# Weight buffers that start 96 bytes apart, and every second weight tile taken in pieces of 256 columns

## The chip, the core and the metric

The kernel runs on one core of a Trainium2 chip. The metric is the device time of one launch in microseconds (us), the median of three runs. A profile of one further execution is read beside it: it records every instruction on TensorE (PE, and PEld for its weight loads), VectorE (DVE), ScalarE (ACT), GpSimd (POOL) and the DMAs that SyncE (SP) issues.

## What is computed

Two layers over 512 tokens of width 1024. Each layer projects the normed tokens into three branches (a latent attention, a state-space scan and an attention over the keys that a top-256 of index scores picks), gates and merges them, and adds a per-layer embedding:

```python
for i in range(DEPTH):                                   # DEPTH = 2
    h = rms_norm(x, norm_g[i])
    (c_q, c_kv, ..., merge_logits) = jnp.split(h @ w_in[i], split_at, axis=-1)
    o_a = mla_branch(...) * jax.nn.silu(gate_a)
    o_b = ssd_branch(...)
    o_c = dsa_branch(...) * jax.nn.silu(gate_c)          # lax.top_k(index_score, 256) inside
    g_a, g_b, g_c = jnp.split(jax.nn.sigmoid(merge_logits), 3, axis=-1)
    merged = g_a * (o_a @ w_br_a[i]) + g_b * (o_b @ w_br_b[i]) + g_c * (o_c @ w_br_c[i])
    x = x + merged @ w_out[i]
    x = x + jax.nn.sigmoid(x @ w_ple_gate[i]) * (p[i] @ w_ple[i])
return rms_norm(x, final_norm)
```

## The kernel before

**The products with weights.** Features lie on partitions, the 512 tokens along the free axis. A unit of weights (128 x 1024 numbers, 512 KB) is fetched by `wload` (L214 to L228) into a buffer `raw`; ACT rounds it to `hi` (L226) and DVE takes the rest, `lo` = raw - hi (L227). Activations are split into `hi` and `lo` the same way. `mm` (L230) makes one tile of results: for each of its k blocks of 128 rows it multiplies hi by hi (L237) and lo by hi (L238), and then hi by lo (L245), all into one PSUM tile. A tile with eight blocks is 24 matmuls, each a 128 x 128 block of weights that stays in the array and 512 token columns that stream past it. Each matmul brings a weight load of its own. In rows, `p<-s,wh` means: into PSUM tile p, streaming s, with wh in the array.

**How much of it there is.** `mm` makes 250 tiles, 244 of 512 columns and six of 256 (the last three `pgate` tiles of layer 1, in two halves each). They are 4,932 of the 7,004 matmuls of the program; `three` (L675) makes another 144 of the same kind without `mm`. The others are the attentions' logits (L779 to L781, L883, L884), their transposes (L563) and products with values (L602), the index scores (L840, L841), the scan (L1009, L1047, L1071, L1076) and small ones.

**The order.** PE's order is the order in which the code is written. `weave` (L487) runs an attention or the scan step by step, and after each step takes some of the tiles' matmuls, four at a time (`CHUNK`), so that PE has work while DVE and ACT do a softmax. The first part of a layer, up to the end of the scan, is such a mixture. After the scan come the last gates, 8 tiles of `br_b`, 8 of `w_out` and 8 of `pgate`, and there tile follows tile with hardly anything between (in the profile from 587 to 740 us and from 1285 to 1432 us). The order on DVE, ACT, POOL and SP is made by a scheduler that puts each instruction where, by its own estimate of times, it could start; `wload`'s three instructions are given priority (`AHEAD`). The buffers are handed out in turn: three `hi`, three `lo`, two `raw` (`WB`).

**The top-256.** `topk` (L854) takes 16 rounds of MAX (L861) and MATCH_REPLACE (L864) on DVE for three blocks of queries, then makes masks (L868). The sparse attention `dsa` needs these masks from its second block on; meanwhile PE runs tiles.

**Places in memory.** All activation tiles are 2,048 bytes a partition and all weight buffers 4,096, and all of them begin at a multiple of 512 bytes. `vc`, the values of the sparse attention (stationary in L602, `p<-s,vc`), begins 160 bytes past one; the other attention's values are ordinary activation tiles (L602, `p<-s,s`).

Of the kernel before, what the change touches and what calls it, by code (L numbers as in the profile page):

```python
# [26 lines left out]
F32R = mybir.dt.float32r  # L27
# [5 lines left out]
L, D, T = 2, 1024, 512  # L33
# [125 lines left out]
class Build:  # L159
    def __init__(self, tc, I, out, ctx, dbg=None):  # L160
        self.tc, self.nc, self.I, self.out, self.dbg = tc, tc.nc, I, out, dbg or {}
        pool = lambda name, **k: ctx.enter_context(tc.tile_pool(name=name, **k))

        self.front = pool("front", bufs=1)
        self.slots = pool("slots", bufs=1)
        self.wp = pool("wp", bufs=2)
        self.const = pool("const", bufs=1)
        self.small = pool("small", bufs=6)
        PS = bass.MemoryType.PSUM
        self.psum = pool("psum", bufs=2, space=PS)  # L170
        self.dram = pool("dram", bufs=1, space=bass.MemoryType.DRAM)
        self.free_slots = deque(range(NSLOT))
        self.todo = deque()
        self.of = {}
        self.n = 0
        self.ahead = 0
        self.fetched = {}
        self.chunk = CHUNK
        self.peak = 0


    def slot(self, dt=F32, shape=(128, 512)):
        i = self.free_slots.popleft()
        self.peak = max(self.peak, NSLOT - len(self.free_slots))
        self.n += 1
# [28 lines left out]
    def wload(self, l, name):  # L214
        if (l, name) in self.fetched:
            return self.fetched.pop((l, name))
        nc = self.nc
        kind, (cols,) = UNITS[UIDX[name]]
        n = 640 if kind == "uq" else _KT[kind] * len(cols)
        hi = self.wp.tile([128, 1024], F32R, name=f"wh{self.n}", tag="whi", bufs=WB[0])  # L220
        lo = self.wp.tile([128, 1024], F32R, name=f"wl{self.n}", tag="wlo", bufs=WB[1])
        raw = self.wp.tile([128, 1024], F32, name=f"wr{self.n}", tag="raw", bufs=WB[2])
        self.n += 1
        with self.tc.high_priority(offset=self.ahead):
            nc.sync.dma_start(raw[:, :n], self.I["w"][l, UIDX[name], :, :n])
            nc.scalar.activation(hi[:, :n], raw[:, :n], AF.Copy)  # L226
            nc.vector.tensor_sub(lo[:, :n], raw[:, :n], hi[:, :n].bitcast(F32))  # L227
        return hi, lo  # L228

    def mm(self, ps, w, off, acts, t=slice(0, T)):  # L230

        nc = self.nc
        hi, lo = w
        n, cost = len(acts), 0
        for k, (ah, al) in enumerate(acts):
            c = slice(off + 128 * k, off + 128 * k + 128)
            nc.tensor.matmul(ps[:, t], hi[:, c], ah[:, t], start=k == 0, stop=False)  # L237
            nc.tensor.matmul(ps[:, t], lo[:, c], ah[:, t], start=False, stop=False)  # L238
            cost += 2
            if cost >= self.chunk:  # L240
                yield cost
                cost = 0
        for k, (ah, al) in enumerate(acts):
            c = slice(off + 128 * k, off + 128 * k + 128)
            nc.tensor.matmul(ps[:, t], hi[:, c], al[:, t], start=False, stop=k == n - 1)  # L245
            cost += 1
            if cost >= self.chunk or k == n - 1:
                yield cost
                cost = 0
# [885 lines left out]
    def layer(self, l, xs, s):  # L1135
# [117 lines left out]

        for m in range(8 - LAST):
            self.pgate(l, m, x1, x1p)
            self.stat_add(s, x1[m], m == 0)
        ws = [self.wload(l, ("pgate", m)) for m in range(8 - LAST, 8)]
        rest = deque()

        def tail(half):  # L1260
# [3 lines left out]
            with self.tc.high_priority(offset=URGENT):  # L1264
                self.pgate(l, 7, x1, x1p, ws[LAST - 1], t)
                nc.scalar.activation(q[:, t], x1[7][:, t], AF.Square)
# [5 lines left out]
        for half in range(2):  # L1272
            t = slice(256 * half, 256 * half + 256)
            for m in range(8 - LAST, 7):
                self.pgate(l, m, x1, x1p, ws[m - 8 + LAST], t)
                self.stat_add(s, x1[m], False, t)
                if half and m == 8 - LAST:
                    R = self.stat_rows(y, range(2))
# [57 lines left out]
REL = (1, 3, 4, 4)  # L1336
WB = (3, 3, 2)
NSLOT = 80
LAST = 3
CHUNK = 4  # L1340
FIRST = (("c_kv", 0), ("c_kv", 1), "C")
# [36 lines left out]
```

## Time and profile before

| | |
|---|---|
| median of three runs (lowest to highest) | 1455.37 us (1454.93 to 1456.69) |
| the profiled execution, its own time | 1455.85 us |
| its span, first to last instruction | 1454.0 us |
| PE, PEld busy | 1410.4 us (97%), 1153.9 us (79%) |
| DVE, ACT, POOL busy | 1092.3 us (75%), 718.8 us (49%), 150.2 us (10%) |
| mean granted TensorE clock | 0.994 of 2.4 GHz |

Busy times of PE are to be read with care: matmuls overlap in the pipeline and their ends are modelled, so that a busy PE need not be at its best. What one matmul costs is the distance between the starts of two that follow each other. A number in square brackets in a row is the idle time of that engine before the instruction, with what ended it.

### The profile page before, as it was taken

To read this page: it belongs to the slowest core of one execution; us is meant where nothing else is said; L and a number is where in the kernel's file an instruction comes from. 1 tells how busy PE (TensorE), PEld (TensorE's weight loads), DVE (VectorE), ACT (ScalarE), POOL (GpSimd) and SP (SyncE) were. 2 spreads that over 40 slices of the span, in tenths; PEclk is the share of its full clock that TensorE was granted. 3 is DMA by queue.
4 is the path that set the end of the run, shared out by engine and by line. 5 is a ranking of instruction groups with operands and counts; after the bars stand their busy time and mean duration, and the time that the engine had idled before them with its cause. 6 is when DMAs were issued, how large, how long until landed. Compare 5 with 4: busy or idle time off the path is not lost.

```text
span 1454.0 us, 20141 instructions
## 1 busy us (share of the span) xinstructions
PE 1410.4 (97%) x7252; PEld 1153.9 (79%) x7252; DVE 1092.3 (75%) x2234; ACT 718.8 (49%) x1367; POOL 150.2 (10%) x140
## 2 busy tenths in 40 slices
PE   6999999998999999999999999999999999999997
PEld 4878877787878778888888888888788777788886
DVE  7668786996888997664565697889888798765545
ACT  7557678525656442432345576632466544342332
POOL 1000000031120221000001000000322122110000
PEclk9999999999999999999999999999999999999998
DMA  7442332433333322543444322323333333244331
GB/s 258 145 130 72 92 97 78 133 103 99 112 113 115 118 80 77 160 153 104 130 160 129 94 75 76 95 91 101 109 105 116 105 115 100 73 132 152 108 101 59
DMA packets 67609, 162.39 MB, mean 112 GB/s; under 512 B 9237, under 2 KB 21653, under 8 KB 67509
## 3 DMA queue, kind: packets, MB, share of 16 engines
q1 hardware_dynamic: 67509, 161.11, 35.5%
q8 instruction: 57, 0.93, 0.3%
q14 instruction: 43, 0.35, 0.1%
HBM read 142.27 MB, written 13.83 MB: 107 GB/s over the span
## 4 chain that ended last, share of the span: by engine, by line
PE 73%; DVE 18%; ACT 3%; issue 3%; DMA 1%; POOL 1%; SPq 0%; POOLq 0%; DVEq 0%; ACTq 0%
PE p L245 20%; PE p L237 19%; PE p L238 19%; DVE wl L227 3%; PE p L602 3%; PE p L563 2%; DVE s L864 2%; DVE s L1034 2%; DVE m L861 2%; ACT wh L226 1%; DVE s L966 1%; DMA s<-cum_d 1%; DVE s L1037 1%; PE p L683 1%; PE p L687 1%
## 5 line engine op out<-in xcount | busy, mean ns | idle before, releaser
L237 PE MATMUL p<-s,wh 128*128 128x512 f32 (+1 forms) x1644 | 650.5, 397 | 9.0 <-ACT wh L226 7.9
L238 PE MATMUL p<-s,wl 128*128 128x512 f32 (+1 forms) x1644 | 637.9, 389 | 1.2 <-DVE wl L227 1.2
L245 PE MATMUL p<-s,wh 128*128 128x512 f32 (+1 forms) x1644 | 425.5, 391 | 0.0
L226 ACT ACTIVATE wh<-wr 128x1024 fp32r<-128x1024 f32 (+2 forms) x214 | 223.6, 1045 | 330.7 <-PE p L245 214.0
L237 PEld LDWEIGHTS p<-s,wh 128*128 128x128 f32 x1644 | 311.3, 189 | 69.6 <-ACT wh L226 7.9
L238 PEld LDWEIGHTS p<-s,wl 128*128 128x128 f32 x1644 | 311.1, 189 | 61.1 <-DVE wl L227 2.6
L245 PEld LDWEIGHTS p<-s,wh 128*128 128x128 f32 x1644 | 300.6, 189 | 59.9 <-issue 2.8
L227 DVE TENSOR_TENSOR wl<-wr,wh 128x1024 fp32r<-128x1024 f32 (+2 forms) x214 | 263.4, 1231 | 108.8 <-ACT wh L226 107.8
L553 ACT ACTIVATE s<-s,m 128x128 f32<-128x128 f32 (+3 forms) x128 | 71.5, 559 | 68.9 <-DVE m L552 68.5
L572 ACT ACTIVATE s<-p 128x256 fp32r<-128x256 f32 (+1 forms) x192 | 65.8, 343 | 56.1 <-PE p L563 27.7
L573 DVE TENSOR_TENSOR s<-p,s 128x256 fp32r<-128x256 f32 (+1 forms) x192 | 71.6, 374 | 14.1 <-ACT s L572 12.7
L881 POOL TENSOR_TENSOR s<-s,s 128x256 f32<-128x256 f32 (+2 forms) x48 | 57.7, 1216 | 134.0 <-DMA s<-bias_d 84.7
L563 PE MATMUL p<-c,s 128*128 128x128 f32 x320 | 56.6, 274 | 7.9 <-DVE s L555 7.9
L563 PEld LDWEIGHTS p<-c,s 128*128 128x128 f32 x320 | 40.4, 140 | 25.4 <-issue 12.8
L1130 DVE SCALAR_TENSOR_TENSOR s<-s,p 128x512 f32<-128x512 f32 x48 | 32.4, 676 | 32.6 <-PE p L245 32.6
L410 ACT ACTIVATE s<-s 128x512 f32<-128x512 f32 (+1 forms) x42 | 25.3, 610 | 63.7 <-DVE s L1097 39.8
L555 DVE TENSOR_SCALAR s<-s,m 128x128 f32<-128x128 f32 (+3 forms) x128 | 52.3, 409 | 2.6
L966 DVE SCALAR_TENSOR_TENSOR s<-p,v,s 128x511 f32<-128x511 f32 (+2 forms) x72 | 53.2, 739 | 0.0
L864 DVE MATCH_REPLACE8 s<-m,s 128x256 f32<-128x256 f32 (+2 forms) x96 | 51.3, 538 | 0.0
L431 POOL TENSOR_TENSOR m<-m,v 128x4 f32<-128x4 f32 (+1 forms) x10 | 12.5, 1247 | 368.4 <-DVE m L430 368.3
L881 POOL TENSOR_TENSOR s<-s,c 128x128 f32<-128x128 f32 x16 | 11.0, 693 | 374.6 <-DMA s<-bias_d 204.4
L861 DVE MAX8 m<-s 128x8 f32<-128x256 f32 (+2 forms) x96 | 49.0, 543 | 0.0
(188 smaller groups left out, 1688.3 us busy)
## 6 DMA issues: line engine op xcount, KB each, us to landing
wr<-in_w_dram SPq DMA_DIRECT2D x204, 512.0 KB, 3.5
s<-cum_d SPq DMA_DIRECT2D x32, 256.0 KB, 3.7
s<-in_x_dram SPq DMA_DIRECT2D x16, 256.0 KB, 4.7
ple_d<-s SPq DMA_DIRECT2D x16, 256.0 KB, 4.0
s<-bias_d SPq DMA_DIRECT2D x16, 256.0 KB, 3.3
s<-ple_d SPq DMA_DIRECT2D x13, 256.0 KB, 2.7
s<-bias_d SPq DMA_DIRECT2D x16, 192.0 KB, 2.7
s<-s SPq DMA_DIRECT2D x44, 64.0 KB, 2.0
```

Source lines behind the costliest of these rows:

```text
L226: nc.scalar.activation(hi[:, :n], raw[:, :n], AF.Copy)
L227: nc.vector.tensor_sub(lo[:, :n], raw[:, :n], hi[:, :n].bitcast(F32))
L237: nc.tensor.matmul(ps[:, t], hi[:, c], ah[:, t], start=k == 0, stop=False)
L238: nc.tensor.matmul(ps[:, t], lo[:, c], ah[:, t], start=False, stop=False)
L245: nc.tensor.matmul(ps[:, t], hi[:, c], al[:, t], start=False, stop=k == n - 1)
L553: nc.scalar.activation(u[:, :n], u[:, :n], AF.Exp, bias=mx, scale=-1.0, accum_out=sm)
L563: nc.tensor.transpose(tp[:, 128 * kb:128 * kb + 128], u[:, 128 * kb:128 * kb + 128], self.ident)
L573: nc.vector.tensor_sub(l_, src, h_.bitcast(F32))
L861: i = nc.vector.max(m8, sc[qt][:, :n])
L864: nc.vector.match_replace(sc[qt][:, :n], m8, sc[qt][:, :n], GONE)
L881: nc.gpsimd.tensor_tensor(b[:, :n], b[:, :n], mask, OP.add)
L966: nc.vector.scalar_tensor_tensor(a[:, d:], ps[:, :T - d], w(3 - d), a[:, d:], op0=OP.mult, op1=OP.add)
```

## The change

A weight buffer gets 24 more columns (`STEP`), 96 bytes. The six begin then at 0, 96, 192, 288, 384 and 480 bytes past a multiple of 512; `raw` and what lies behind it move by 64 bytes. The activation tiles stay where they were. And `mm` counts its tiles: of every second one each matmul is issued as two of 256 columns with the same weights (`wide`). The first tile is one of these.

```diff
+        self.tiles = 0
...
-        hi = self.wp.tile([128, 1024], F32R, name=f"wh{self.n}", tag="whi", bufs=WB[0])
-        lo = self.wp.tile([128, 1024], F32R, name=f"wl{self.n}", tag="wlo", bufs=WB[1])
+        hi = self.wp.tile([128, 1024 + STEP], F32R, name=f"wh{self.n}", tag="whi", bufs=WB[0])
+        lo = self.wp.tile([128, 1024 + STEP], F32R, name=f"wl{self.n}", tag="wlo", bufs=WB[1])
...
+    def wide(self, ps, w, a, t, first=False, last=False):
+        for i in range(t.start, t.stop, self.piece):
+            s = slice(i, min(i + self.piece, t.stop))
+            self.nc.tensor.matmul(ps[:, s], w, a[:, s], start=first and i == t.start, stop=last, skip_group_check=True)
...
+        self.tiles += 1
+        piece = T >> self.tiles % 2
         for k, (ah, al) in enumerate(acts):
             c = slice(off + 128 * k, off + 128 * k + 128)
-            nc.tensor.matmul(ps[:, t], hi[:, c], ah[:, t], start=k == 0, stop=False)
-            nc.tensor.matmul(ps[:, t], lo[:, c], ah[:, t], start=False, stop=False)
+            self.piece = piece
+            self.wide(ps, hi[:, c], ah, t, first=k == 0)
+            self.wide(ps, lo[:, c], ah, t)
...
-            nc.tensor.matmul(ps[:, t], hi[:, c], al[:, t], start=False, stop=k == n - 1)
+            self.piece = piece
+            self.wide(ps, hi[:, c], al, t, last=k == n - 1)
...
+STEP = 24
```

In the built program 121 of the 244 wide tiles are split: 2,310 matmuls become 4,620, and the program has 9,314 matmuls in place of 7,004. The 2,310 stand, by the place of their predecessors in the trace of before, so: 329 between 587 and 740 us and 306 between 1285 and 1432 us, where tile follows tile, and 1,675 in the mixtures. Of these, 161 stand between 254 and 330 us, 104 between 480 and 546 us, 144 between 970 and 1038 us and 98 between 1180 and 1245 us. The order of PE's tiles does not change. On PE, at a tile boundary of `br_b` in layer 0 (p is the PSUM tile, wh and wl the weights in the array), before:

```order
L245 MATMUL p_6397<-s_418,wh_6391 128x512
L245 MATMUL p_6397<-s_423,wh_6391 128x512
L245 MATMUL p_6397<-s_428,wh_6391 128x512
L237 MATMUL p_6430<-s_392,wh_6424 128x512
L238 MATMUL p_6430<-s_392,wl_6425 128x512
```

and after:

```order
L236 MATMUL p_7252<-s_442,wh_7246 128x256 x2
L236 MATMUL p_7252<-s_447,wh_7246 128x256 x2
L236 MATMUL p_7252<-s_452,wh_7246 128x256 x2
L236 MATMUL p_7309<-s_416,wh_7303 128x512
L236 MATMUL p_7309<-s_416,wl_7304 128x512
```

The matmuls stand in the same places, those of the first tile twice. On DVE the scheduler makes some hundred small moves. One is at the end of the top-256 of layer 0, where the masks (L868, after the change L880) wait for the last MATCH_REPLACE. Before:

```order
L861 MAX m_3702<-s_1282 128x8
L864 MATCH_REPLACE s_1281<-m_3699,s_1281 128x384
L864 MATCH_REPLACE s_1282<-m_3702,s_1282 128x512
L1130 SCALAR_TENSOR_TENSOR s_2800<-s_2800,p_3646 128x512
L227 TENSOR_TENSOR wl_3762<-wr_3763,wh_3761 128x1024
L868 TENSOR_SCALAR s_1280<-s_1280 128x256
L868 TENSOR_SCALAR s_1281<-s_1281 128x384
L868 TENSOR_SCALAR s_1282<-s_1282 128x512
```

and after:

```order
L873 MAX m_4121<-s_1426 128x8
L1142 SCALAR_TENSOR_TENSOR s_2958<-s_2958,p_4010 128x512
L876 MATCH_REPLACE s_1426<-m_4121,s_1426 128x512
L880 TENSOR_SCALAR s_1424<-s_1424 128x256
L880 TENSOR_SCALAR s_1425<-s_1425 128x384
L880 TENSOR_SCALAR s_1426<-s_1426 128x512
L924 TENSOR_TENSOR s_4263<-s_764,hv 128x64
L925 SCALAR_TENSOR_TENSOR s_4263<-s_4263 128x64
L1142 SCALAR_TENSOR_TENSOR s_3055<-s_3055,p_4045 128x512
L938 TENSOR_SCALAR m_4281<-s_4263 128x64
L228 TENSOR_TENSOR wl_4185<-wr_4186,wh_4184 128x1024
```

The masks come ahead of a branch's result and a weight unit's `lo` that stood before them.

## Rows read from the trace of the kernel before

**Rows 1.** The page, engines: busy us (share of the span) and instructions.

```profile
PE 1410.4 (97%) x7252; PEld 1153.9 (79%) x7252; DVE 1092.3 (75%) x2234; ACT 718.8 (49%) x1367; POOL 150.2 (10%) x140
```

**Rows 2.** The timeline, PE, a whole tile of pgate in layer 0: start us, duration us.

```profile
699.92 0.39 PE L237 MATMUL p<-s,wh 128*128 128x512 f32 x1
...
705.36 0.39 PE L237 MATMUL p<-s,wh 128*128 128x512 f32 x1
```

**Rows 3.** The timeline, PE, a tile of 256 columns near the end.

```profile
1426.95 0.28 PE L237 MATMUL p<-s,wh 128*128 128x256 f32 x1
1427.07 0.28 PE L238 MATMUL p<-s,wl 128*128 128x256 f32 x1
...
1428.87 1.12 PE L245 MATMUL p<-s,wh 128*128 128x256 f32 x8
1429.83 0.28 PE L422 MATMUL p<-c,s 128*128 128x1 f32 x2
```

**Rows 4.** The timeline, PEld, weight loads of the same tile.

```profile
1426.83 0.19 PEld L237 LDWEIGHTS p<-s,wh 128*128 128x128 f32 x1
1426.95 0.19 PEld L238 LDWEIGHTS p<-s,wl 128*128 128x128 f32 x1
```

**Rows 5.** Groups by line and shape, PEld: busy us, mean ns | idle before.

```profile
L883 PEld LDWEIGHTS p<-s,s 128*128 128x128 f32 x64 | 12.0, 188 | 2.8
L884 PEld LDWEIGHTS p<-s,s 128*128 128x128 f32 x64 | 12.0, 188 | 2.6
```

**Rows 6.** The timeline, PE, tiles mixed with the sparse attention of layer 0.

```profile
406.21 0.28 PE L883 MATMUL p<-s,s 128*128 128x256 f32 x1
406.32 0.28 PE L884 MATMUL p<-s,s 128*128 128x256 f32 x1
406.44 0.40 PE L237 MATMUL p<-s,wh 128*128 128x512 f32 x1
...
408.27 0.60 PE L563 MATMUL p<-c,s 128*128 128x128 f32 x4
...
409.87 0.40 PE L237 MATMUL p<-s,wh 128*128 128x512 f32 x1
...
411.72 0.27 PE L563 MATMUL p<-c,s 128*128 128x128 f32 x1
411.75 1.20 PE L602 MATMUL p<-s,vc 128*128 128x256 f32 x8
412.78 1.09 PE L245 MATMUL p<-s,wh 128*128 128x512 f32 x4
```

**Rows 7.** Line 602: duration ns min/median/max, first and last start us, forms.

```profile
L602 PEld LDWEIGHTS p<-s,s x192: 186/189/193, 116.2 to 964.6; 128*128 128x128 f32 x192
L602 PE MATMUL p<-s,s x192: 277/282/387, 116.2 to 964.7; 128*128 128x256 f32 x192
L602 PEld LDWEIGHTS p<-s,vc x192: 186/188/193, 342.8 to 1156.2; 128*128 128x128 f32 x192
L602 PE MATMUL p<-s,vc x192: 276/281/388, 342.9 to 1156.3; 128*128 128x256 f32 x192
```

**Rows 8.** Stretches: us, busy of PE, PEld, DVE, ACT, POOL, clock, DMA, GB/s.

```profile
250.00:330.00 80.00, 80.00 (x480) 63.27 (x479) 79.43 (x190) 29.36 (x60) 11.99 (x11) 1.00 0.39 116
330.00:480.00 150.00, 143.60 (x729) 118.32 (x728) 123.06 (x289) 87.54 (x192) 25.76 (x24) 0.99 0.35 112
970.00:1040.00 70.00, 68.72 (x310) 56.62 (x308) 67.48 (x167) 20.36 (x31) 11.62 (x10) 1.00 0.35 108
```

**Rows 9.** The timeline, PE, where it waits in and after these stretches.

```profile
333.81 0.45 PE L563 MATMUL p<-c,s 128*128 128x128 f32 x1 [3.38 <-DVE s L555]
1039.68 0.52 PE L563 MATMUL p<-c,s 128*128 128x128 f32 x3 [1.28 <-DVE s L555]
```

**Rows 10.** Groups by line and shape, PE: busy us, mean ns | idle, releaser.

```profile
L563 PE MATMUL p<-c,s 128*128 128x128 f32 x320 | 56.6, 274 | 7.9 <-DVE s L555 7.9
...
L1009 PE MATMUL p<-s,s 128*128 128x512 f32 x24 | 13.4, 643 | 4.0 <-POOL s L1053 4.0
```

## The prediction

> **What bounds the kernel now.** I read the engines' busy time first [rows 1]: PE 97%, DVE 75%, the rest less. Since a busy PE need not be at its best, I then went to the timeline and took distances between starts. Where tile follows tile, 24 matmuls of 512 columns take 705.36 - 699.92 = 5.44 us, 226.7 ns each, with no gap [rows 2]. A tile of 256 columns near the end takes 1429.83 - 1426.95 = 2.88 us, 120.0 ns each [rows 3]. The difference, 106.7 ns, is what 256 columns cost, so 512 columns cost 213.3 ns, and 13.3 ns of every matmul are a fixed price that doesn't depend on its width. That is the number this change turns on. PE waits for others only in few places: the two largest I could tie to another engine's long work are 3.38 us and 1.28 us after the top-256 of each layer [rows 9], in stretches where DVE is busy 79.43 of 80 and 67.48 of 70 us [rows 8], and two waits of about 2 us in the scan (4.0 us together) [rows 10]. So PE's own work sets the end nearly everywhere, and what is added to it is paid unless it falls ahead of such a wait.
>
> **The pieces, where tile follows tile.** 2,310 matmuls are each made two of half the width. The columns are the same, so the price is one more fixed price each, if a piece costs what the narrow tiles of before cost. The weights are loaded again for the second piece: L883 and L884 already use the same stationary block one after the other, and each has its own 64 loads [rows 5]. That load is hidden: in the narrow tile it starts with the matmul ahead (load at 1426.95 for the matmul at 1427.07) and the matmuls still start every 120 ns [rows 3, 4]. So 635 x 13.3 ns = 8.4 us, with nothing to hide it, since PE waits for nobody there.
>
> **The pieces, in the mixtures.** Here the same kinds cost other distances, because the matmul before was of another kind. Eight matmuls of 512 columns take 408.27 - 406.44 = 1.83 us, 229 ns each; another eight take 411.72 - 409.87 = 1.85 us, 231 ns [rows 6]. Narrow ones are a little cheaper than 120 ns: a transpose and eight narrow matmuls take 412.78 - 411.72 = 1.06 us; with 0.11 us for the transpose that is 119 ns each, and the pair L883, L884 takes 406.44 - 406.21 = 0.23 us, 115 ns each. So the price of a split lies between 2 x 115 - 230 = 0 ns (the pair) and 13.3 ns (the settled train), with 2 x 119 - 230 = 8 ns for a train of eight. Four matmuls at a time become eight pieces, so the train of eight is the nearest row; pieces that follow longer settle towards 13.3. I take 10 ns: 1,675 x 10 ns = 16.8 us, with 0 and 22.3 us as ends. Sum on PE: 8.4 + 16.8 = 25.2 us, from 8.4 to 30.7.
>
> A rule of the Trainium skill speaks for less. The page "TensorE: Matmul & The Clock Gate", section Back-to-back issue gap, gives columns / 2.4 GHz and about 2.5 ns more as the distance of two matmuls; by it the 2,310 pieces would add 5.8 us. The rows show 13.3 ns in place of 2.5, so the trace disagrees for matmuls that each bring a weight load, and the sum goes by the rows.
>
> **What the waits take back.** In the stretch from 250 to 330 us DVE sets the pace and 161 of the split matmuls lie there: 1.6 us more on PE shorten the wait of 3.38 us by as much. The wait is followed by a dip of the clock (0.99 in the stretch from 330 us on, 1% of 150 us = 1.5 us lost) [rows 8, 9]; with a shorter wait it may go. In layer 1, 144 matmuls, 1.4 us, go ahead of the wait of 1.28 us, which I take as gone. The two waits of 2 us in the scan shrink by at most what is added while DVE is full ahead of them, 104 and 98 matmuls, 1 us each. PE's other waits for a softmax ahead of its transposes are 7.9 - 3.38 - 1.28 = 3.2 us [rows 9, 10]; I let half of it, 1.5 us, be taken, an estimate. Sum: 1.6 + 1.3 + 2 + 1.5 = 6.4, with half of the dip 7 us; ends 2 and 10. What is late next after the top-256 is PE itself.
>
> **The starts of the weight buffers.** If the place within 512 bytes mattered to a weight load or to the stream beside it, L602 would show it, because it runs the same matmul with weights at 0 bytes (s) and at 160 bytes past a multiple of 512 (vc). Loads take 189 and 188 ns, matmuls 282 and 281 ns in the median [rows 7]. I take nothing for it. No row shows ACT's and DVE's rounding of a unit at another start; they lie beside PE's work, and only where DVE is full could a slower one show. As ends I keep +/-2 us.
>
> **The scheduler's moves.** On PE nothing moves. On DVE the masks come out earlier at the end of layer 0's top-256; the branch's result and the `lo` that now follow them are needed later. The work ahead of the softmax that PE waits for stays the same, so I count nothing and keep +/-3 us for the hundred small moves.
>
> Sum against the profiled execution: 1455.85 + 25.2 - 7 = 1474. The median of the runs lies 0.5 us lower: 1473.5 us, 1.2% slower.
>
> **The rivals.**
> (a) The full price: every extra piece costs 13.3 ns also in the mixtures, and only 2 us are hidden. For it: settled trains, which are the longest rows; against it: [rows 6]. 1455.4 + 30.7 - 2 = 1484 us.
> (b) The second piece is almost free in the mixtures, as in the pair L883, L884, which has the same form: 8.4 + 0 to 3 us, less 5 hidden: 1460 us. Against it: the train of eight is nearer.
> (c) The other side, faster. The 13.3 ns may be a meeting of the next block's load with the stream, since both begin at the same place within 512; other starts would lower it to f for all 7,386 matmuls of this kind (4,932 + 144 + 2,310). The change is then 7,386 f - 5,076 x 13.3 ns, and it gains once f is under 9.1 ns. At half, f = 6.7, it is 18 us: 1437 us. Against it: vc starts elsewhere and costs the same [rows 7]. For it: vc has one such place, not six.
> (d) The starts do harm: a load that crosses a multiple of 512 takes longer, and a piece of 120 ns has less room to hide it than a matmul of 227 ns. 10 ns on each of the 4,620 pieces are 46 us: 1520 us. Against it: vc's loads cross too.
> (e) The change doesn't do what it says: no second load for the same weights, and no second fixed price. Then the sum is about nothing and the waits stay: 1455 us. Against it: 64 and 64 loads [rows 5].
> (f) The second load isn't hidden behind a matmul of the same rows. 2,310 loads of 0.19 us [rows 4] are 0.43 ms: 1890 us. The same rows show a load that runs beside a matmul, so this has next to no chance. The Trainium skill's page "TensorE: Matmul & The Clock Gate", section The mechanism of Part 3 (Packing small matmuls), says that a load overlaps a running matmul only where their row groups differ; the trace disagrees here, for both use all 128 rows.
>
> **How the numbers follow.** Forecast 0.62 (1466 to 1481), (a) 0.13, (b) 0.13, (c) 0.05, (d) 0.03, (e) 0.03, (f) 0.01. From 1460 to 1485 lies the forecast, (a) and most of (b), about 0.83. Within 0.2% (2.9 us, about what a measurement of this kernel can tell from no change) fall (e) and a little of (b): 0.04. Faster: (c), 0.05. Slower: 0.91.
>
> **What would show it.** In the profile after: some 9,560 matmuls and as many loads (7,252 + 2,310); where tile follows tile, tiles of 24 that alternate between 5.44 and 5.76 us; the wait after the first top-256 down to about 1.8 us; rounding on ACT and DVE as long as before; weight loads still 188 ns. Wrong would be: a wide tile that no longer takes 5.44 us (the starts matter), a split one outside 5.7 to 5.8 us, or an alternation that shows but a total that doesn't follow it.

## The result, and the profile after

The changed kernel takes 1469.37 us, the median of four runs (1468.72 to 1470.98), against 1455.15 us of four runs of before: 1.01 times as long, with a 95% interval of 1.0088 to 1.0113. It is slower by 14.2 us; the forecast was 18. The profiled execution (1468.72 us) has a span of 1466.9 us, 12.9 more than before. Its page begins so (engines: busy us, share of the span, instructions), and the second view gives the granted clock, which was 0.994 before:

```profile
span 1466.9 us, 24775 instructions
PE 1431.9 (98%) x9562; PEld 1270.2 (87%) x9562; DVE 1097.7 (75%) x2234; ACT 719.2 (49%) x1367; POOL 148.6 (10%) x140
...
core 0: 1466.9 us, clock 0.997
```

There are 2,310 matmuls more than in [rows 1], and as many weight loads more. (In both kernels the profile counts 248 more matmuls than the built program has.) A weight load in `mm` still takes 188 ns in the median, and the rounding of a unit 1.06 us on ACT and 1.22 us on DVE, as before. PE is the only engine that got visibly more work. In the groups of PE by line and shape (busy us, mean ns | idle before, releaser) the transposes, L575, now wait 1.6 us where they waited 7.9 [rows 10], and the scan's matmul, L1021, waits 2.7 us instead of 4.0:

```profile
L236 PE MATMUL p<-s,wh 128*128 128x512 f32 x1652 | 550.4, 399 | 1.1 <-ACT s L409 1.1
L236 PE MATMUL p<-s,wh 128*128 128x256 f32 x3176 | 540.1, 284 | 8.2 <-ACT wh L227 8.2
...
L575 PE MATMUL p<-c,s 128*128 128x128 f32 x320 | 56.4, 274 | 1.6 <-DVE s L567 1.5
...
L1021 PE MATMUL p<-s,s 128*128 128x512 f32 x24 | 12.5, 602 | 2.7 <-POOL s L1065 2.7
```

The next rows are PE's timeline in `pgate` of layer 0 (start us, duration us). A split tile lies between the first and the third row, a wide one between the third and the last. The last matmuls of a tile and the first of the next have one name and are merged, so I measure from each tile's first matmul with `wl` to the next tile's:

```profile
700.09 0.40 PE L236 MATMUL p<-s,wl 128*128 128x256 f32 x2
...
703.64 2.27 PE L236 MATMUL p<-s,wh 128*128 128x256 f32 x17
705.74 0.39 PE L236 MATMUL p<-s,wl 128*128 128x512 f32 x1
...
709.19 2.23 PE L236 MATMUL p<-s,wh 128*128 128x512 f32 x10
711.26 0.40 PE L236 MATMUL p<-s,wl 128*128 128x256 f32 x2
```

The split tile takes 5.65 us where I expected 5.76, and the wide one 5.52 us, where it took 5.44 before [rows 2]. Both were on my list of what would be wrong: a split tile outside 5.7 to 5.8 us, and a wide tile that no longer takes 5.44 us, which means that the starts matter.

To see where the 12.9 us come from, I matched every matmul with weights to its predecessor in the trace of before and compared the starts. The stretches are named by the times of before; the numbers are us more or less than before.

| stretch | split in the change | changed kernel | e1 starts alone | e2 pieces alone | e10 |
|---|---|---|---|---|---|
| 0 to 254 | 281 | +3.6 | +2.5 | +3.0 | +3.0 |
| 254 to 337, top-256 and the wait behind it | 166 | -2.9 | +0.3 | -2.8 | -1.3 |
| 337 to 587 | 397 | +1.4 | +1.0 | +3.1 | +1.6 |
| 587 to 740, tile after tile | 329 | +4.7 | +3.4 | +4.5 | +0.1 |
| 740 to 970 | 297 | +3.1 | +2.2 | +3.0 | +1.8 |
| 970 to 1043, top-256 and the wait | 148 | +1.6 | +0.7 | +1.6 | +2.2 |
| 1043 to 1285 | 386 | -1.4 | -0.7 | -1.1 | -3.1 |
| 1285 to 1429, tile after tile | 306 | +4.1 | +3.2 | +4.1 | -0.2 |
| from 1429 | 0 | -1.4 | -0.4 | -1.3 | +1.3 |
| sum | 2,310 | +12.9 | +12.2 | +14.2 | +5.3 |

The starts alone cost nearly as much as the pieces alone, and the two together no more than the pieces. That needed experiments. Two things are asked: what the place of the buffers does to a matmul, and where the sum of the extra work went.

### The profile page after: what moved, and what is told of

It is laid out like the page before. It is cut to its first block, busy times and chain, and to the rows that moved or that the text cites. A ratio compares the mean times of both kernels' runs of the same rounds, so it can differ in the third digit from the quotient of the medians.

```text
span 1466.9 us, 24775 instructions
## 1 busy us (share of the span) xinstructions
PE 1431.9 (98%) x9562; PEld 1270.2 (87%) x9562; DVE 1097.7 (75%) x2234; ACT 719.2 (49%) x1367; POOL 148.6 (10%) x140
## 4 chain that ended last, share of the span: by engine, by line
PE 74%; DVE 18%; issue 3%; ACT 2%; DMA 2%; POOL 1%; SPq 0%; POOLq 0%; DVEq 0%; ACTq 0%
PE p L236 59%; DVE wl L228 3%; PE p L614 3%; PE p L575 2%; DVE s L978 2%; DVE s L876 2%; DVE s L1046 2%; DVE m L873 1%; DVE s L1049 1%; ACT wh L227 1%; DMA s<-cum_d 1%; PE p L699 1%; PE p L695 1%; PE p L793 1%; PE p L791 1%
## 5 line engine op out<-in xcount | busy, mean ns | idle before, releaser
L236 PE MATMUL p<-s,wh 128*128 128x256 f32 (+1 forms) x4828 | 1065.4, 323 | 9.3 <-ACT wh L227 8.2
L236 PEld LDWEIGHTS p<-s,wh 128*128 128x128 f32 x4828 | 753.5, 189 | 82.6 <-ACT wh L227 8.2
L236 PE MATMUL p<-s,wl 128*128 128x256 f32 (+1 forms) x2414 | 646.5, 321 | 1.2 <-DVE wl L228 1.2
L236 PEld LDWEIGHTS p<-s,wl 128*128 128x128 f32 x2414 | 401.1, 189 | 30.9 <-DVE wl L228 2.1
L575 PE MATMUL p<-c,s 128*128 128x128 f32 x320 | 56.4, 274 | 1.6 <-DVE s L567 1.5
L567 DVE TENSOR_SCALAR s<-s,m 128x128 f32<-128x128 f32 (+3 forms) x128 | 56.0, 437 | 2.5
L575 PEld LDWEIGHTS p<-c,s 128*128 128x128 f32 x320 | 39.7, 140 | 13.8 <-issue 5.4
L265 DVE TENSOR_TENSOR s<-s,s 128x512 fp32r<-128x512 f32 (+1 forms) x58 | 43.5, 751 | 8.9 <-ACT s L264 8.7
L264 ACT ACTIVATE s<-s 128x512 fp32r<-128x512 f32 (+1 forms) x58 | 36.3, 626 | 26.0 <-DVE s L657 10.3
L461 DVE SCALAR_TENSOR_TENSOR s<-s,v,p 128x512 f32<-128x512 f32 x42 | 29.0, 743 | 26.2 <-PE p L450 26.2
```

The costliest lines, as they stand in the source:

```text
L236: self.nc.tensor.matmul(ps[:, s], w, a[:, s], start=first and i == t.start, stop=last, skip_group_check=True)
L567: nc.vector.tensor_scalar(u[:, :n], u[:, :n], rs, None, op0=OP.mult)
L575: nc.tensor.transpose(tp[:, 128 * kb:128 * kb + 128], u[:, 128 * kb:128 * kb + 128], self.ident)
```

## Experiments: the starts and the pieces apart

By "settled" I mean a matmul behind at least twelve of the same width in a row; the numbers are means over all such distances between starts that hold no wait and no dip of the clock (under 250 ns for wide ones, under 132 for narrow ones; 2,480 wide ones in the trace of before: 226.7 ns; 104 narrow ones: 119.9 ns). In the changed kernel they are 231.2 and 118.3 ns.

**e1, the starts alone.**

```diff
-        piece = T >> self.tiles % 2
+        piece = T
```

> The six starts alone, no pieces: every tile is 512 columns wide again. After the change a wide matmul well inside a tile took 231 ns where it took 226.7 before, and a narrow one 118.3 where it took 119.9. Theory S (the starts do both): wide matmuls stay at 231 ns here; between br_b and the end of layer 0 (153.0 us before, 668 such matmuls) that is 3.0 us more, and the whole comes to 1462 to 1467 us. Theory A (the alternation of widths does it, the starts nothing): 226.7 ns, 153.0 us, 1455 us as before.

Measured: 1.0079 of before (1.0064 to 1.0094), median 1467.74 us. Settled wide matmuls 232.2 ns, a little more than theory S had. PE's timeline, one wide tile of `pgate`, 706.34 - 700.74 = 5.60 us:

```profile
700.74 0.40 PE L236 MATMUL p<-s,wl 128*128 128x512 f32 x1
...
704.24 2.26 PE L236 MATMUL p<-s,wh 128*128 128x512 f32 x9
706.34 0.40 PE L236 MATMUL p<-s,wl 128*128 128x512 f32 x1
```

The alternation of widths falls as a cause: there is none here. The starts lengthen wide matmuls by 5.5 ns.

**e2, the pieces alone.**

```diff
-STEP = 24
+STEP = 0
```

> The pieces alone, all buffers at a multiple of 512 again. Theory S: wide matmuls 226.7 ns, narrow ones 119.9, so 13.1 ns for each split one; 329 of them between br_b and the end of layer 0 add 4.3 us there, and the whole lies within 3 us of the changed kernel, since what the starts add on wide tiles they take back on narrow ones. Theory A: as the changed kernel in each stretch, 231 and 118.3 ns, 1469 us.

Measured: 1.0103 (1.0087 to 1.0119), median 1470.56 us. A split tile takes 706.77 - 701.02 = 5.75 us and the wide one behind it 712.24 - 706.77 = 5.47 us; settled, 120.0 and 226.7 ns. The 0.03 us above 5.44 in the wide tile are its first matmuls, which still settle after the change of width.

```profile
701.02 0.40 PE L236 MATMUL p<-s,wl 128*128 128x256 f32 x2
...
706.77 0.40 PE L236 MATMUL p<-s,wl 128*128 128x512 f32 x1
...
712.24 0.40 PE L236 MATMUL p<-s,wl 128*128 128x256 f32 x2
```

So with buffers at multiples of 512 every distance is as the rows of before said, and the pieces do what the forecast's first part says.

**e4, six starts and every tile in pieces.**

```diff
-        piece = T >> self.tiles % 2
+        piece = T >> 1
```

> Six starts and every tile in pieces: 4,788 extra matmuls instead of 2,310 and no alternation of widths. Theory S: narrow matmuls stay at 118.3 ns, so 9.9 ns a split one against 226.7, 6.6 us between br_b and the end of layer 0, and some 1455 + 40 - 10 = 1485 us in all. Theory A: without alternation they settle at 119.9 ns, 13.1 ns a split one, 8.8 us there and about 1500 us.

Measured: 1.0162 (1.0146 to 1.0179), median 1479.53 us; narrow matmuls settle at 118.3 ns, and a tile takes 706.40 - 700.72 = 5.68 us. The total is 5 us under theory S's. The shorter narrow matmul belongs to the starts, not to the alternation. The price of another 2,478 pieces is 10 us.

```profile
700.72 0.40 PE L236 MATMUL p<-s,wl 128*128 128x256 f32 x2
...
704.26 2.31 PE L236 MATMUL p<-s,wh 128*128 128x256 f32 x18
...
706.40 0.40 PE L236 MATMUL p<-s,wl 128*128 128x256 f32 x2
```

## Experiments: which place

**e3, one shift for all six buffers**, 96 bytes past a multiple of 512, no pieces (the buffers stay apart by a multiple of 512).

```diff
+STEP = 128
-        hi = self.wp.tile([128, 1024 + STEP], ..., tag="whi", bufs=WB[0])
+        hi = self.wp.tile([128, 1024 + STEP], ..., tag="whi", bufs=WB[0])[:, 24:24 + 1024]
...
```

> No pieces; all six buffers are read and written 96 bytes past a multiple of 512, so that they differ from the activations but not from each other. Theory S1 (what counts is a weight block's place against the stream's): wide matmuls at about 231 ns as with six starts, 1462 to 1467 us. Theory S2 (what counts is that blocks which follow each other start at different places): 226.7 ns, 1455 us. Theory A: 1455 us.

Measured: 1.0127 (1.0107 to 1.0146), median 1472.94 us; settled wide matmuls 234.3 ns, a tile 709.14 - 703.52 = 5.62 us. Both the distance and the total lie above theory S1's. That the six differ from each other is not needed; a start that differs from the activations' is enough.

```profile
703.52 0.40 PE L236 MATMUL p<-s,wl 128*128 128x512 f32 x1
...
707.04 2.27 PE L236 MATMUL p<-s,wh 128*128 128x512 f32 x9
709.14 0.40 PE L236 MATMUL p<-s,wl 128*128 128x512 f32 x1
```

**e7, everything 96 bytes later**, the activation tiles too (the first tile of the partition is made 24 columns longer; `STEP` is 0, no pieces).

> All tiles of the partition, the activations too, begin 96 bytes later: weights and streams stand to each other as before. Theory R (the place of the weights against the stream counts): 226.7 ns, 153.0 us between br_b and the end of layer 0, 1455 us. Theory P (a place by itself counts, for a load or a stream): as with the one shift, 234 ns, 157.8 us there, 1470 us.

Measured: 1453.52 us in one execution, settled 226.7 ns, a tile 700.44 - 695.00 = 5.44 us. The weights begin at the same 96 bytes as in e3, and nothing is lost. So it is the place of the weights against the stream that counts.

```profile
695.00 0.39 PE L236 MATMUL p<-s,wl 128*128 128x512 f32 x1
...
698.40 2.20 PE L236 MATMUL p<-s,wh 128*128 128x512 f32 x9
700.44 0.39 PE L236 MATMUL p<-s,wl 128*128 128x512 f32 x1
```

**e5 and e6, one shift of 256 bytes and one of 64** (as e3, with columns 64 and 16 in place of 24).

> As the one shift of 96 bytes, but 256. There settled wide matmuls took 234.3 ns instead of 226.7. Theory M (only a start at a multiple of 512, where a 512-byte block of weights covers whole units, keeps the short distance): about 234 ns here too, 1470 us. Theory F (a finer grid, 64 or 128 bytes, counts): 226.7 ns, 1455 us.

> As the one shift of 96 bytes, but 64. Theory M: about 234 ns for settled wide matmuls, 1470 us. Theory F with a grid of 64: 226.7 ns, 1455 us. If 256 keeps the short distance and 64 doesn't, the grid lies between.

Measured, one execution each: at 256 bytes 1455.42 us and 226.7 ns, a tile 700.64 - 695.20 = 5.44 us, all as at 0. At 64 bytes 1466.72 us; wide matmuls settle at 233.3 ns (705.71 - 700.11 = 5.60 us), but the narrow ones at the end of the kernel at 113.3 ns: the tile in the last three rows takes 1437.67 - 1434.95 = 2.72 us, 2.88 before [rows 3].

```profile
695.20 0.39 PE L236 MATMUL p<-s,wl 128*128 128x512 f32 x1
...
700.64 0.39 PE L236 MATMUL p<-s,wl 128*128 128x512 f32 x1
```

```profile
700.11 0.39 PE L236 MATMUL p<-s,wl 128*128 128x512 f32 x1
...
705.71 0.39 PE L236 MATMUL p<-s,wl 128*128 128x512 f32 x1
...
1434.95 0.28 PE L236 MATMUL p<-s,wh 128*128 128x256 f32 x1
...
1436.54 1.18 PE L236 MATMUL p<-s,wh 128*128 128x256 f32 x9
1437.67 0.28 PE L236 MATMUL p<-s,wh 128*128 128x256 f32 x1
```

Neither theory M nor a grid of 64 holds. A shift of 256 counts as none, and 64 is a place of its own: wide matmuls pay more there, narrow ones less.

**e9, eight places in one kernel.** Each unit of weights is put 0, 32, ... 224 bytes past a multiple of 512 in turn; eight tiles in pieces alternate with eight wide ones.

```diff
-        piece = T >> self.tiles % 2
+        piece = T >> self.tiles // 8 % 2
...
+        o = 8 * (self.units % 8)
+        self.units += 1
-        hi = self.wp.tile([128, 1024 + STEP], ..., tag="whi", bufs=WB[0])
+        hi = self.wp.tile([128, 1024 + STEP], ..., tag="whi", bufs=WB[0])[:, o:o + 1024]
...
```

> A look at the price of a matmul by the place of its weights: each unit of weights is put 0, 32, 64, ... 224 bytes past a multiple of 512 in turn, hi and lo alike, and eight tiles in pieces alternate with eight wide ones. Known from uniform shifts, settled: wide 226.7 ns at 0, 233.3 at 64, 234.3 at 96; narrow 119.9, 113.3, 118.3. Theory L (the load of the next block and the stream meet in a pattern that repeats every 256 bytes, and some place avoids the meeting): one of the untried places gives narrow ones of 107 to 110 ns or wide ones under 224. Theory N (the fixed price can be shifted between the widths, not lost): narrow ones stay over 113 and wide ones over 226 everywhere. The total time says nothing here beyond lying between 1460 and 1490 us.

Measured, 1475.41 us in one execution; means of the settled distances by place (here at least twelve of the same width and place stand before), 52 to 91 wide and 266 to 317 narrow ones each:

| bytes past a multiple of 512 | 0 | 32 | 64 | 96 | 128 | 160 | 192 | 224 |
|---|---|---|---|---|---|---|---|---|
| wide, 512 columns, ns | 226.6 | 233.5 | 233.5 | 234.1 | 233.5 | 233.4 | 228.8 | 233.2 |
| narrow, 256 columns, ns | 120.0 | 118.3 | 115.2 | 118.0 | 118.8 | 119.9 | 117.4 | 117.2 |

No place is cheaper than 0 for wide matmuls, and none makes a pair of narrow ones (226.6 ns at the best, in e6) clearly cheaper than a wide one at 0. Of the two theories N holds in the means, as far as 32-byte steps show it. The table also fits the change: over its six places (0, 32, 96, 128, 192 and 224 bytes past a multiple of 256) the means are 231.6 ns for wide matmuls and 118.3 for narrow ones, where e1 has 232.2 and e4 118.3.

**e10, one shift of 64 bytes and every tile in pieces.** It takes the two best numbers together.

> All six buffers 64 bytes past a multiple of 512 and every tile in pieces, 4,788 extra matmuls. With six starts the same pieces cost 118.3 ns each and the kernel 1479.5 us. If a narrow matmul's price is set by the place (113.3 ns settled at 64), a pair takes 226.6 ns, as much as a wide one at 0: between br_b and the end of layer 0 153.0 us as before, and in all 1449 to 1458 us, the lower end if the clock dips behind PE's waits go as they did with pieces alone. If the 113 ns belong to the few narrow matmuls at the end of the kernel and don't hold with the mass of them, 118 ns and 1475 us or more.

Measured: 1.0018 (1.0005 to 1.0031), median 1457.73 us of twelve runs. A tile of 48 pieces takes 703.55 - 698.12 = 5.43 us, as long as 24 wide ones before:

```profile
698.12 0.39 PE L236 MATMUL p<-s,wl 128*128 128x256 f32 x2
...
701.51 2.20 PE L236 MATMUL p<-s,wh 128*128 128x256 f32 x18
...
703.55 0.39 PE L236 MATMUL p<-s,wl 128*128 128x256 f32 x2
```

With the same 4,788 extra matmuls and loads as e4, it is 22 us faster; the place alone does that. The last column of the table of stretches shows it in both stretches where tile follows tile. Its sum of +5.3 us is of a profiled execution that took 1461.12 us, 3.4 us over the median. Where tiles are mixed with other work a pair still costs some 2.6 ns more than a wide matmul, and the total stays above before by a little, not below as I had hoped.

The 113.3 ns are not the price of the place alone. In this kernel, at the same 64 bytes, settled narrow matmuls keep one of two distances, train by train: of 6,021, 3,994 lie at 113 to 115 ns and 2,026 at 117 ns or more. This tile of 48 pieces takes 325.27 - 319.62 = 5.65 us, 117.7 ns each:

```profile
319.62 0.40 PE L236 MATMUL p<-s,wl 128*128 128x256 f32 x2
...
323.15 2.28 PE L236 MATMUL p<-s,wh 128*128 128x256 f32 x18
325.27 0.40 PE L236 MATMUL p<-s,wl 128*128 128x256 f32 x2
```

What decides between the two isn't shown. The 115.2 ns in the table by place are a mean over both.

## Experiment: where the extra work is hidden

**e8, pieces only ahead of waits**, with buffers at multiples of 512: in the top-256 of layer 0 and in the end of the sparse attention and the scan of layer 1.

```diff
-        piece = T >> self.tiles % 2
+        piece = T >> self.cut
...
+        self.cut = int(l == 0)
         self.weave(tk, TOP[1], work, ...)
+        self.cut = 0
...
+        self.cut = int(l == 1)
         self.weave(group0(), 16, ...)
```

> Buffers at multiples of 512; pieces only in three stretches, the top-256 of layer 0, and the end of the sparse attention with the scan of layer 1. With pieces alone the first stretch grew by 2.1 us, but the wait behind it shrank by 4.8 us, half of it by a clock dip that went; the last two came out 2 to 3 us shorter. Theory H (extra work ahead of a wait is hidden and keeps the clock up): 4 to 7 us less than before, 1449 to 1452 us, clock 0.996 or more. Theory O (the dips and waits went by the scheduler's moves on DVE in all the kernel): no gain, 1455 to 1460 us.

Measured: 0.9991 (0.9982 to 1.0000), median 1454.62 us of eleven runs; no gain that can be told from none. In the profile, whose span is 1451.4 us against 1454.0, the 768 extra matmuls are paid back and a little more: the stretch from 254 to 330 us grows by 3.3 us, and the next, with the wait, shrinks by 4.9 us, the clock's dip with it. In the scan of layer 1 the waits of 1.9 and 2.0 us shrink to nothing and 0.3 us, and from 1043 to 1285 us it is 1.4 us shorter. But from 480 to 546 us, in the scan of layer 0, where nothing was split, it is 1.4 us longer: the clock dips at 543 us instead, behind a wait of 2.02 us, where none followed the same wait of 2.01 us before. It isn't the scheduler: in the built programs the order on DVE, ACT, POOL and SP is that of before from 331 to 1166 us. Theory H holds for the waits that the pieces stand ahead of, not for the total.

## Why the forecast came out near, step by step

**The price of a piece: right.** To separate price from waits I summed the differences of all distances that hold no wait (under 250 ns for a wide matmul, under 132 for a narrow one or a piece). In e2 that gives 12.97 ns for each of the split matmuls where tile follows tile (I said 13.3), and 10.2 ns in the mixtures (I took 10, between 0 and 13.3). That is 24.2 us, and 26.5 us in all with 2.3 us that the whole matmuls pay, which the forecast did not have; my sum was 25.2. The train of eight, to which I gave most weight [rows 6], was the right row, and the pair L883, L884 the wrong one. The rule of the Trainium skill that the prediction set against the rows (page "TensorE: Matmul & The Clock Gate", section Back-to-back issue gap) is given there for a matmul by itself; for a stream in which every matmul has its load the section says that both set the distance. So the 13.3 ns of the rows do not contradict its 2.5.

**The starts: wrong.** I took nothing, and they alone cost 12.2 us in the profile. In the changed kernel this is hidden because it works on both sides. By the same sum, its 26.8 us consist of 18.1 us on the split matmuls (9.6 and 7.7 ns each instead of 13.0 and 10.2) and 8.7 us on whole ones (4.3 and 2.9 ns each). Against e2 the starts make the whole matmuls dearer by 6.4 us and the pieces cheaper by 6.1 us, and that my total stood is luck. The row I relied on, vc at 160 bytes [rows 7], was true and did not answer the question: L602 is 256 columns wide, and e9 shows that at 160 bytes a narrow matmul takes 119.9 ns, as at 0 (120.0), while a wide one takes 233.4 instead of 226.6. I had one width and one place, and both happened to be the case that shows nothing.

Rival (c) looked in the right place, the start of the weights against the stream, but had the wrong sign for wide matmuls: the fixed price of 13.3 ns went up for them (to 21 ns at 96 bytes) and down for narrow ones (to 6.6 at 64, in part of the trains). That it is a meeting of the load with the stream isn't shown. Rival (d) had the sign for wide matmuls, but loads that cross a multiple of 512 are not the reason: in e7 they cross, and nothing is lost, and a load takes 188 ns in the median, as before.

**What the waits take back: too small.** Against 26.8 us of price the span grew by 12.9, so 13.9 were taken back; I had 7, with 10 as the end. Two terms were mis-sized. The first is the waits, 6.4 us in the forecast. By the two pages PE's idle time, span less busy time, fell from 43.6 to 35.0 us, 8.6 less. Its transposes wait 6.3 us less (7.9 to 1.6) and the scan's matmul 1.3 us less, but some comes back elsewhere: L614 waits 3.0 us for DVE, where L602 waited 1.4 before. The wait of 1.28 us after the top-256 of layer 1, which I took as gone, is 0.73 us. The wait of 3.38 us after the first one [rows 9] did not fall to 1.8 us: it is gone. Before, from the first MAX of this top-256 to the start of DVE's result that PE waits for:

```profile
250.53 0.43 DVE L861 MAX8 m<-s 128x8 f32<-128x256 f32 x1
...
333.37 0.29 DVE L555 TENSOR_SCALAR s<-s,m 128x128 f32<-128x128 f32 x1
```

and after, with PE's transpose, which has no wait before it:

```profile
254.03 0.43 DVE L873 MAX8 m<-s 128x8 f32<-128x256 f32 x1
...
335.42 0.29 DVE L567 TENSOR_SCALAR s<-s,m 128x128 f32<-128x128 f32 x1
...
335.76 0.33 PE L575 MATMUL p<-c,s 128*128 128x128 f32 x1
```

PE comes to the transpose 335.76 - 254.03 = 81.73 us after the MAX; before it was 333.81 - 3.38 - 250.53 = 79.90. That is 1.8 us more work, where I had 1.6. And DVE's result starts 81.39 us after the MAX in place of 82.84, 1.45 us earlier. This I had at nothing ("the work ahead of the softmax that PE waits for stays the same"). It goes with the scheduler's moves on DVE: in e2, which has the same moves, it is 81.40 us, and in e1, whose order is that of before, 82.87. Which of the moves does it isn't shown.

The second term is the clock. I counted half of one dip; three went, 1.7 us each, 5.1 us. With the 8.6 us of waits that is 13.7 of the 13.9 us. The stretches (columns as in [rows 8]) of the changed kernel, and then of e1, where the waits stayed long, show 17 us around the first wait and 22 us around the scan's:

```profile
333.00:350.00 17.00, 16.28 (x113) 14.68 (x112) 12.77 (x33) 10.84 (x28) 2.58 (x3) 1.00 0.41 134
1240.00:1262.00 22.00, 20.62 (x120) 17.11 (x119) 21.64 (x38) 8.99 (x14) 3.51 (x3) 1.00 0.29 101
```

```profile
333.00:350.00 17.00, 14.14 (x64) 11.20 (x63) 11.01 (x29) 9.74 (x24) 2.65 (x3) 0.90 0.38 121
1240.00:1262.00 22.00, 20.13 (x81) 15.12 (x81) 19.68 (x35) 8.41 (x13) 3.99 (x3) 0.92 0.26 83
```

A clock of 0.90 over 17 us and of 0.92 over 22 us is 1.7 us lost each, as it was in the trace of before. The third dip lies at the end, where nothing is split and yet 1.4 us were gained. Before, the narrow matmuls behind the statistics' wait stood 0.21 us apart, at the lower of the two clock levels (granted clock 0.50 from 1433.0 to 1435.4 us); in the changed kernel, behind a wait as long (1.73 us before it, 1.72 in the trace of before), 0.12 us (granted clock 1.00 from 1446.9 to 1449.5 us). Before:

```profile
1433.13 0.41 PE L238 MATMUL p<-s,wl 128*128 128x256 f32 x1
1433.35 0.41 PE L237 MATMUL p<-s,wh 128*128 128x256 f32 x1
```

and after:

```profile
1446.97 0.28 PE L236 MATMUL p<-s,wl 128*128 128x256 f32 x1
1447.09 0.29 PE L236 MATMUL p<-s,wh 128*128 128x256 f32 x1
```

Why equal waits bring a dip in one kernel and none in the other, no run here shows; in the profiled execution of e3, without pieces but with slower matmuls, all three were gone too, and in that of e1 all three stayed. It isn't the kernel alone: the mean clock of single executions goes from 0.994 to 0.997 in e1 and from 0.994 to 0.998 in e10. Yet it is 0.996 or 0.997 in all four of the changed kernel and never over 0.995 before, so this term is not one execution's chance.

**The other rivals.** (a) asked for 13.3 ns everywhere and little hidden, (b) for free pieces in the mixtures: e2 has 10.2 ns. (e) falls with the 9,562 loads, and (f) with tiles of 5.65 us. The scheduler's moves I had at nothing, +/-3 us; the 1.45 us after the first top-256 are the one share that these runs show.

## What to carry to other kernels

A matmul that loads its own weights pays a fixed price, here 13 ns, and that price depends on how the weights and the stream lie to each other in memory: keep both at the same place within 256 bytes when the stream is 512 columns wide, and measure before giving that up. Splitting a matmul costs one such price where the engine never waits, and here somewhat less where it runs other kinds in between (10.2 ns); the waits, and the clock that falls behind them, gave back half of the sum here. A row that shows "no difference" answers for its own width and place only, so ask of it whether it would have shown one.

## What the runs showed of the hardware that I had not expected

The distance of two matmuls depends on the start of the weights relative to the streamed tile, modulo 256 bytes as far as tried: 226.7 ns at 0 and 256, 233.3 at 64 and 234.3 at 96 for 512 columns; 119.9 at 0, 113.3 at 64 (in e10 117.7 in a third of the cases) and 118.3 at 96 for 256 columns. With both operands moved by 96 bytes it is 226.7 again. That the reads of load and stream hinder each other would explain it, but the trace shows only the distances. The Trainium skill's page "TensorE: Matmul & The Clock Gate", section Step-by-step, says that loading the next weights "doesn't steal SBUF read bandwidth from the running matmul". These runs neither confirm nor refute that: e3 and e7 differ by 7.6 ns a matmul by the relative place alone, while a load takes 188 ns in both, and through what the place acts isn't shown.

At 64 bytes a narrow matmul's whole price over its columns (106.7 ns) is 6.6 ns, or 11 in the other trains; at 0 it is 13.3; for wide ones it is 20.0 and 13.3. Why one width gains what the other loses stays open.
